# A decoder layer with seven-product matrix multiplication: sums of weights made ahead of time for one more pair of chunks

## The chip, the cores and the metric

The kernel runs on one core of one Trainium2 chip. The metric is the device time of one execution in microseconds (us), as the median of several runs; lower is better. A profile is one further execution, recorded instruction by instruction. The engines of the core are TensorE (PE: matmuls; PEld: its weight loads), VectorE (DVE), ScalarE (ACT), GpSimd (POOL) and SyncE (SP, which here only issues transfers).

## The reference

One layer over 256 tokens of width 2048, all in float32: a SwiGLU feed-forward (inner width 5632), a token mixer, a cross-attention, a second SwiGLU feed-forward, a final norm.

```python
def swiglu(h, w_gate, w_up, w_down):
    return (jax.nn.silu(h @ w_gate) * (h @ w_up)) @ w_down

...
x = x + 0.5 * swiglu(rms_norm(x, ffn1_norm[l]), ffn1_w_gate[l], ffn1_w_up[l], ffn1_w_down[l])
x = gated_parallel_mixer(x, ...)      # window attention || RWKV-7 time mixing
x = memory_cross_attention(x, ...)
x = x + 0.5 * swiglu(rms_norm(x, ffn2_norm[l]), ffn2_w_gate[l], ffn2_w_up[l], ffn2_w_down[l])
...
# in the time mixing:
kk = k * k_k
kk = kk / jnp.maximum(jnp.sqrt(jnp.sum(kk * kk, axis=-1, keepdims=True)), 1e-12)   # removal keys
```

## The kernel before

**Products of split numbers.** Every large product has float32 operands. Each operand is split into a high part, rounded to the fast matmul type (float32r), and a low part, what is left; a product is three matmuls: high x high, low x high, high x low (`times`, L417 to L419). For weights, ACT makes the high part (`hi`, L344) and VectorE the low part (`lo`, L345). TensorE holds 128 x 128 of the activations and streams 512 columns of weights.

**Items.** Weights come in items of `KU` = 2 chunks of 128 rows by 512 columns. `weight_plan` lists all of them in the order of use; `next_item` loads ahead (`load`, L336, on SP's queue), splits two items ahead (`divide`) and hands over the next. In the mixer a load is 512 KB, into one of four `raw` tiles; in the feed-forwards it is 1024 KB (`raw2`, also four).

**Seven products.** Gate and up of the same 512 columns, or two column blocks of down, are done together (`product_pair`). A pair of chunks, two column blocks and two token blocks make a 2 x 2 by 2 x 2 block product: eight products plainly, seven in the Strassen-Winograd way, with sums of activations (`combinations`) and sums of weights. `SEVEN = (0, 2, 4)` says that of the eight pairs of chunks of a gate-and-up block, the pairs 0, 2 and 4 are done with seven. For those, `divide` makes four differences on VectorE (L371 to L374) into two `raw` tiles, and splits them (`two_parts`, L352 on ACT, L353 on VectorE) into `thi`/`tlo`, of which there is one set for the first sum and one for the second. One row of the up weights is then not needed by itself.

The second feed-forward has one gate-and-up block done plainly (j = 0) and ten later ones done in pairs, in three groups of columns, each followed by its down products.

**The mixer** runs a fixed list of products (queries, keys, the small vectors, removal and attention gates, receptances and values, the late gates, then the projections), and between their matmuls the steps of background generators: `product` calls `bg.tick()` twice per item, and each tick lets the first generators of each group take one step to their next `yield`. `idle(n)` is n ticks of waiting. `removal_keys` sums squares over a head with a full-precision matmul by `bdones` (L1022), `substitute` solves small triangular systems step by step on VectorE, `pairs` is the chain of masked products (L1190 to L1306), `finish` makes the features `yr` that the product by `w_proj_rwkv` needs. Large mixer tiles come from one ring of 23, `t4`: a new tile waits until the tile that had its place is done with.

**Order.** Instructions of each engine run in the order in which they stand in the program. That order is fixed when the program is made, by a scheduler that follows the order above and moves an instruction ahead of another that it expects to wait. A transfer on SP's queue waits for its own semaphores, and everything behind it on that queue waits too.

Of the kernel before, what the change touches and what calls it, by code (L numbers as in the profile page):

```python
# [7 lines left out]
F32 = mybir.dt.float32  # L8
# [27 lines left out]


SEVEN, SEVEN_DOWN = (0, 2, 4), ((2, 4, 6), (2, 4))


# [40 lines left out]
def feed_forward_plan(wg, wu, wd, last):  # L81
    for j0, nj in GROUPS:
        for j in range(j0, j0 + nj):
            if j == 0:
                for w in (wg, wu):
                    yield w, 0, KD, 0, 512
            else:
                yield (wg, wu), 0, KD, (j * 512, j * 512), SEVEN
        yield (wd, wd), 4 * j0, 4 * nj, (0, 512), SEVEN_DOWN[nj < 4]
        if last and (j0, nj) == GROUPS[-1]:  # L90
            for n in (2, 3):
                yield wd, 4 * j0, 4 * nj, n * 512, 512
        else:
            yield (wd, wd), 4 * j0, 4 * nj, (1024, 1536), SEVEN_DOWN[1]
# [38 lines left out]
def decoder_layer(ctx: ExitStack, tc: tile.TileContext, a: dict, out: bass.AP):  # L133
# [15 lines left out]
    bg.group("norm", 1)  # L149
    bg.group("mem", 1)  # L150

    def f32(x):
# [34 lines left out]
    select(ident[:], ones[:], [[-1, P]], ALU.is_equal, 0.0, 0, 1)  # L187
    bdup = cpool.tile([P, 2, P], F32, name="bdup")[:, 0, :]
    center = cpool.tile([P, P], F32, name="center")

    def mixer_constants(sp):

        abias = sp.tile([P, 2, P], F32, name="abias")
        pool.memset(abias[:], 0.0)
        select(abias[:, 0, :], abias[:, 0, :], [[1, P]], ALU.is_gt, NEG, 0, -1)
        select(abias[:, 1, :], abias[:, 1, :], [[-1, P]], ALU.is_ge, NEG, 0, 1)

        ups = sp.tile([P, 2, P], F32, name="ups")[:, 0, :]
# [7 lines left out]
        select(mask_l[:], ups, [[-1, P]], ALU.is_gt, 0.0, 0, 1)  # L206
        bdones = sp.tile([P, P], F32, name="bdones")
# [3 lines left out]
        pool.memset(bdup, 0.0)  # L211
# [6 lines left out]
        keep = sp.tile([P, 2, P], F32, name="keep")  # L218
# [7 lines left out]
        return abias, mask3, mask_l, bdones, ones_r, keep  # L226

# [73 lines left out]

    plan, units, items, ends = [], [], [], []
    for entry in weight_plan(a):
        if entry is None:
            ends.append(len(units))
            continue
        plan.append(entry)
        w, k0, nk, c0, n = entry
        if not isinstance(w, tuple):
            for k in range(k0, k0 + nk, KU):  # L310
                items.append(((len(units),), False))
                units.append((w, k, c0, n))
            continue
        for k in range(k0, k0 + nk, 2 * KU):
            u = len(units)
            units += [(v, k + i, c, 512) for v, c in zip(w, c0) for i in (0, KU)]
            items += [((u + i, u + 2 + i), (k - k0) // KU + i in n) for i in range(2)]
    raws, parts = {}, {}
# [37 lines left out]
    def divide(i):  # L356
# [14 lines left out]
        dve.tensor_tensor(t[1][:, 0], ru[:, 0], rg[:, 0], ALU.subtract)  # L371
        dve.tensor_tensor(t[0][:, 0], ru[:, 1], ru[:, 0], ALU.subtract)
        dve.tensor_tensor(t[0][:, 1], ru[:, 1], t[1][:, 0], ALU.subtract)  # L373
        dve.tensor_tensor(t[1][:, 1], rg[:, 1], t[0][:, 1], ALU.subtract)  # L374
        a_ = two_parts(t[0], "a")
        parts[i] = split_unit(g), split_unit(u, slice(1, 2)), (a_, two_parts(t[1], "b"))

    def next_item():
# [7 lines left out]
        for j in range(i + 1, min(i + 1 + AHEAD, len(items))):  # L386
# [3 lines left out]
            for v in items[j][0]:  # L390
                load(v)
            divide(j)
        return parts[i]

# [33 lines left out]

    def combinations(sp, x: Act, seven, name, ready=lambda: True, early=True):

        pairs = [q for q in range(max(seven) + 1) if early or q in seven]
        n = 12 if not early else sum(4 if q in seven else 2 for q in pairs)
        parts = [sp.tile([P, n, P], F32R, tag=name + e, name=name + e) for e in ("hi", "lo")]
# [222 lines left out]
    def feed_forward(sp, x, norm: Norm, wg, wu, wd, done, begin_last=lambda: None, last=False):  # L658
        if last:
# [8 lines left out]
        c = combinations(  # L668
            sp, norm.x, SEVEN, "c", lambda: norm.r is not None and at["item"] > begun + 4
        )  # L670
        c["next"] = []
        for gi, (j0, nj) in enumerate(GROUPS):
# [3 lines left out]
            )  # L676
            ch = combinations(sp, h, SEVEN_DOWN[nj < 4], "d", early=False)

# [93 lines left out]
    with tc.tile_pool(name="mx", bufs=1, reuse_waits="tile") as sp:  # L772
        aligned(sp)
        abias, mask3, mask_l, bdones, (bdones_r, bdmean), keep = mixer_constants(sp)
# [233 lines left out]
        def removal_keys(h):  # L1008
# [8 lines left out]
            act.activation(sq[:], kk[:], AF.Square)  # L1017
            yield
            for i in (0, 2):
                b = tr()  # L1020
                sq2 = sq[:, i : i + 2, :].rearrange("p c t -> p (c t)")
                pe.matmul(b[:], bdones[:], sq2, start=True, stop=True)  # L1022
                act.activation(sq2, b[:], AF.Sqrt)
# [28 lines left out]
            for c in range(2):  # L1052
# [81 lines left out]
        def values(h):  # L1134
# [13 lines left out]
            for i in (0, 2):  # L1148
                b = head_sums(
                    bdones_r, [v[:, i : i + 2, :].rearrange("p c t -> p (c t)") for v in kp[h]]  # L1150
                )
# [51 lines left out]
        def pairs(h, q):  # L1203
# [11 lines left out]
            for c in range(2):  # L1215
                cs_ = slice(c * P, (c + 1) * P)
                if c == 0:
                    mk = masked(h, js, ((0, 0), (1, 0)))
                    yield
                    later = masked(h, js, ((2, 0), (2, 1)))  # L1220
                    yield
                vp = [vtok[h][:, c, j * P : (j + 1) * P] for j in js]
# [85 lines left out]
                if c == 0:  # L1308
                    s0 = small("s0", "s0", 2)
                    for k, j in enumerate(js):  # L1310
                        dve.scalar_tensor_tensor(
                            s0[:, k, :], b[:, (2 + k) * P : (3 + k) * P], dec[h][:, j : j + 1],
                            bdup, ALU.mult, ALU.mult,
                        )
# [100 lines left out]
        for n in range(4):  # L1415
# [4 lines left out]
            for t in range(2):  # L1420
                dve.tensor_tensor(s[:, t, :], po[t][:], s[:, t, :], ALU.add)
            bg.spawn("feat", n3.block(n, s))
            if n == 0:
# [156 lines left out]
```

## Time and profile before

| | us |
|---|---|
| median of 3 runs | 2251.75 |
| lowest and highest run | 2251.66, 2252.43 |
| the profiled execution | 2252.57 |
| its span, first to last instruction | 2250.8 |

The granted TensorE clock over the span is 0.999. By place in the span, the first feed-forward ends near 745 us, the mixer and the cross-attention near 1520, the second feed-forward with the final norm ends the span. The transfers move 432.49 MB at a mean of 192 GB/s.

In the page's and the views' lines, a row of instructions reads: engine, line of the kernel, operation, output tile `<-` input tiles, shapes, count; then busy time and mean of one. In an order by time, the row begins with its start and its duration in us, and brackets give the idle time of the engine before it and what ended it. Matmuls overlap in the pipe, so their durations are longer than the distance of their starts.

### The profile page before, as it was taken

How to read it: one execution, taken by the hardware profiler on the slowest of the kernel's cores; microseconds unless marked ns; L12 is line 12 of the kernel's file. 1: busy time of each engine (PE TensorE's matmuls, PEld its weight loads, DVE VectorE, ACT ScalarE, POOL GpSimd, SP SyncE). 2: the span in 40 equal slices, each digit the busy share in tenths (PEclk: the TensorE clock that was granted, in tenths of full speed). 3: DMA queues.
4: the chain of work that ended last, by engine and by line, in shares of the span. 5: the costliest groups of instructions: out<-in, count | busy, mean ns of one | idle time of the engine just before them, and what ended most of it. 6: DMA issues, size and time to landing. Idle time of an engine off the chain costs nothing.

```text
span 2250.8 us, 28046 instructions
## 1 busy us (share of the span) xinstructions
PE 2235.2 (99%) x10617; PEld 1840.3 (82%) x10617; DVE 1782.0 (79%) x2279; ACT 1226.5 (54%) x1601; POOL 132.6 (6%) x192
## 2 busy tenths in 40 slices
PE   9999999999999999999999999999999999999998
PEld 7888888888888877788888888888888888888886
DVE  7898988998989476887534566557998988998987
ACT  6555555555556467444444446556555555554554
POOL 1000000000001000301220040001000000000002
PEclk9999999999999999999999999999999999999999
DMA  7555555556556544676523476548565565555564
GB/s 263 187 201 201 197 203 202 193 190 216 192 188 205 163 142 150 201 223 212 166 77 109 163 261 227 186 159 284 185 213 187 195 210 194 190 209 200 189 207 147
DMA packets 219143, 432.49 MB, mean 192 GB/s; under 512 B 14107, under 2 KB 16384, under 8 KB 219008
## 3 DMA queue, kind: packets, MB, share of 16 engines
q1 hardware_dynamic: 210432, 404.78, 53.3%
q0 software_dynamic: 8112, 25.12, 3.5%
q8 instruction: 83, 1.36, 0.2%
q10 hardware_dynamic: 464, 0.79, 0.1%
q14 instruction: 52, 0.43, 0.1%
HBM read 417.56 MB, written 13.11 MB: 191 GB/s over the span
## 4 chain that ended last, share of the span: by engine, by line
PE 94%; DVE 3%; DMA 1%; issue 1%; POOL 1%; ACT 0%; SPq 0%; POOLq 0%; DVEq 0%; ACTq 0%
PE acc L417 19%; PE acc L418 19%; PE acc L419 19%; PE mm L419 8%; PE mm L418 8%; PE mm L417 8%; PE tr L605 2%; PE tr L418 2%; PE tr L419 2%; PE tr L417 2%; PE mm L1254 1%; DVE lo L345 1%; PE tr L1190 1%; DMA raw<-in_w_out_dram 0%; PE mm L844 0%
## 5 line engine op out<-in xcount | busy, mean ns | idle before, releaser
L345 DVE TENSOR_TENSOR lo<-raw,hi 128x1024 fp32r<-128x1024 f32 (+1 forms) x770 | 894.5, 1163 | 336.6 <-ACT hi L344 334.4
L344 ACT CAST hi<-raw 128x1024 fp32r<-128x1024 f32 (+1 forms) x770 | 759.3, 997 | 734.7 <-PE acc L419 519.6
L417 PE MATMUL acc<-hi,xhi 128*128 128x512 f32 (+1 forms) x1196 | 474.3, 397 | 2.4 <-ACT xhi L632 1.9
L418 PE MATMUL acc<-lo,xhi 128*128 128x512 f32 (+1 forms) x1196 | 464.8, 389 | 0.0
L419 PE MATMUL acc<-hi,xlo 128*128 128x512 f32 (+1 forms) x1196 | 464.1, 388 | 0.0
L417 PEld LDWEIGHTS acc<-hi,xhi 128*128 128x128 f32 x1196 | 225.0, 188 | 51.4 <-issue 4.0
L419 PEld LDWEIGHTS acc<-hi,xlo 128*128 128x128 f32 x1196 | 224.5, 188 | 46.9 <-DVE xlo L633 1.0
L418 PEld LDWEIGHTS acc<-lo,xhi 128*128 128x128 f32 x1196 | 224.9, 188 | 45.3 <-issue 1.7
L352 ACT CAST thi<-raw 128x1024 fp32r<-128x1024 f32 x172 | 178.9, 1050 | 60.4 <-DVE raw L373 46.5
L353 DVE TENSOR_TENSOR tlo<-raw,thi 128x1024 fp32r<-128x1024 f32 x172 | 208.3, 1220 | 0.7 <-ACT thi L352 0.4
L417 PE MATMUL mm<-hi,xhi 128*128 128x512 f32 x380 | 149.3, 393 | 0.0
L419 PE MATMUL mm<-hi,xlo 128*128 128x512 f32 x380 | 148.2, 390 | 0.0
L418 PE MATMUL mm<-lo,xhi 128*128 128x512 f32 x380 | 148.2, 390 | 0.0
L418 PE MATMUL acc<-lo,hhi 128*128 128x512 f32 x372 | 145.6, 391 | 0.8 <-DVE lo L345 0.8
L419 PE MATMUL acc<-hi,hlo 128*128 128x512 f32 x372 | 145.6, 391 | 0.0
L417 PE MATMUL acc<-hi,hhi 128*128 128x512 f32 x372 | 144.9, 390 | 0.0
L419 PEld LDWEIGHTS mm<-hi,xlo 128*128 128x128 f32 x380 | 71.3, 188 | 14.8
L418 PEld LDWEIGHTS mm<-lo,xhi 128*128 128x128 f32 x380 | 71.4, 188 | 14.5
L417 PEld LDWEIGHTS mm<-hi,xhi 128*128 128x128 f32 x380 | 71.4, 188 | 14.5
L418 PEld LDWEIGHTS acc<-lo,hhi 128*128 128x128 f32 x372 | 69.9, 188 | 15.5 <-DVE lo L345 1.2
L417 PEld LDWEIGHTS acc<-hi,hhi 128*128 128x128 f32 x372 | 69.9, 188 | 14.3
L419 PEld LDWEIGHTS acc<-hi,hlo 128*128 128x128 f32 x372 | 69.9, 188 | 14.0
(392 smaller groups left out, 3511.9 us busy)
## 6 DMA issues: line engine op xcount, KB each, us to landing
raw<-in_ffn_w_up_dram SPq DMA_DIRECT2D x88, 1024.0 KB, 5.4
raw<-in_ffn_w_down_dram SPq DMA_DIRECT2D x88, 1024.0 KB, 5.1
raw<-in_ffn_w_gate_dram SPq DMA_DIRECT2D x84, 1024.0 KB, 5.1
raw<-in_w_in_dram SPq DMA_DIRECT2D x136, 512.0 KB, 3.5
raw<-in_w_out_dram SPq DMA_DIRECT2D x32, 512.0 KB, 4.5
raw<-in_w_proj_attn_dram SPq DMA_DIRECT2D x16, 512.0 KB, 3.9
raw<-in_w_proj_rwkv_dram SPq DMA_DIRECT2D x16, 512.0 KB, 5.7
raw<-in_w_cross_kv_dram SPq DMA_DIRECT2D x16, 512.0 KB, 3.6
```

Of the source, the lines that this page charges most:

```text
L344: at["hi"] = act.copy(hi[:, s], raw[:, s])
L345: at["lo"] = dve.tensor_tensor(lo[:, s], raw[:, s], f32(hi[:, s]), ALU.subtract)
L352: act.copy(hi[:], v[:])
L353: dve.tensor_tensor(lo[:], v[:], f32(hi[:]), ALU.subtract)
L417: pe.matmul(o, xh, hi, start=first, stop=False, **how)
L418: pe.matmul(o, xh, lo, start=False, stop=False, **how)
L419: pe.matmul(o, xl, hi, start=False, stop=last, **how)
L605: pe.transpose(b[:, o : o + P], tok[:, t, col : col + P], ident[:])
L1190: pe.matmul(b[e][:, o : o + P], x1[r, j, cs_], x2[r, j, cs_], start=True, stop=True)
L1254: pe.matmul(vb[:, (o + k) * P : (o + k + 1) * P][:, r], lhs(k, e), rhs[:, k, r], start=first and k + e == 0, stop=True, **ek,)
```

## The change

Four things are changed.

- In the second feed-forward, the ten later gate-and-up blocks use seven products in the pairs 0, 2, 3 and 4 (`SEVEN_2`) instead of 0, 2 and 4. The sums of activations (`combinations`) grow by two blocks.
- For pair 3 the sums of weights are not made there. Ten generators (`stage`, a background group of its own, up to four at a time), which start during the receptance, value and late gate products at the items in `STAGE_AT`, load the pair's gate and up weights into two `t4` tiles, make the four differences on VectorE, and store the sums to device memory, all transfers on SP's queue. In the second feed-forward `load_sums` brings them back into two `raw` tiles, two items ahead. The row of the up weights that is not used is not loaded.
- `removal_keys` splits the squares (`halves_of`, new tiles `sh` and `sl`) and sums them with the two matmuls of `head_sums` by the float32r `bdones`.
- Steps of the mixer are delayed by ticks (`idle`, `later_by`): the small vectors' shifts, the removal keys, `substitute`, the masks of `pairs`, the norm after `w_out`; the last attention projection does its last items one token block after the other (`skew`); some constants move between pools.

```diff
+SEVEN_2, STAGED = (0, 2, 3, 4), (3,)
+STAGE_AT = [257, 261, 265] + [268 + 2 * n for n in range(7)]
...
-                yield (wg, wu), 0, KD, (j * 512, j * 512), SEVEN
+                yield (wg, wu), 0, KD, (j * 512, j * 512), SEVEN_2 if last else SEVEN
...
+    bg.group("stage", 4)
...
+    def later_by(n, steps):
+        yield from idle(n)
+        yield from steps
...
+            for i in range(2):
+                q = (k - k0) // KU + i
+                if n == SEVEN_2 and q in STAGED:
+                    staged[len(items)] = len(staged)
+                items.append(((u + i, u + 2 + i), q in n))
+    first_unused = {items[i][0][1] for i in staged}
+    sums_d = dram.tile([len(staged), P, 4, 512], F32, name="sums")
...
+        if u in first_unused:
+            second = u + 1 in first_unused
+            pieces = [(slice(1, 2), nc.sync)] + [(slice(2 + second, 4), nc.sync)]
+            if not second:
+                pieces = ((slice(1, 4), nc.sync),)
+        elif u + 1 in first_unused and wide:
+            pieces = ((slice(0, 2), nc.sync), (slice(3, 4), nc.sync))
...
+    def load_sums(i):
+        if i not in staged or i in summed:
+            return
+        summed[i] = [
+            wp.tile([P, KU, 512], F32, tag="raw", name="raw", bufs=4) for _ in range(2)
+        ]
+        for e, t in enumerate(summed[i]):
+            nc.sync.dma_start(t[:], sums_d[staged[i], :, KU * e : KU * e + KU, :])
+
+    def stage(t4, i, n):
+        while at["item"] < STAGE_AT[n]:
+            yield
+        t = t4("su", (P, KU, 512)), t4("sg", (P, KU, 512))
+        for e, v in zip(t, items[i][0][::-1]):
+            w, k, c0, _ = units[v]
+            rows = slice(k * P, (k + KU) * P)
+            nc.sync.dma_start(e[:], w[rows, c0 : c0 + 512].rearrange("(a p) n -> p a n", p=P))
+        yield from idle(4)
+        u0, u1, g0, g1 = (e[:, c] for e in t for c in range(KU))
+        with tc.issue_after(at["lo"].ins):
+            dve.tensor_tensor(g0, u0, g0, ALU.subtract)
+            dve.tensor_tensor(u0, u1, u0, ALU.subtract)
+        yield
+        with tc.issue_after(at["lo"].ins):
+            dve.tensor_tensor(u1, u1, g0, ALU.subtract)
+            dve.tensor_tensor(g1, g1, u1, ALU.subtract)
+        yield from idle(6)
+        for c, e in enumerate(t):
+            nc.sync.dma_start(sums_d[n, :, KU * c : KU * c + KU, :], e[:])
...
-        rg, ru = raws[g], raws[u]
-        t = [wp.tile([P, KU, 512], F32, tag="raw", name="raw", bufs=4) for _ in range(2)]
+        t = summed.get(i)
+        if t is None:
+            rg, ru = raws[g], raws[u]
+            t = [wp.tile([P, KU, 512], F32, tag="raw", name="raw", bufs=4) for _ in range(2)]
...
             for v in items[j][0]:
                 load(v)
+            load_sums(j)
             divide(j)
+        load_sums(i + 2)
...
+        for i, n in staged.items():
+            bg.spawn("stage", stage(t4, i, n))
...
+            if name == "small":
+                yield from idle(2)
...
-            yield
+            sp_ = halves_of(sq[:], t4("sh", dt=F32R)[:], t4("sl", dt=F32R)[:])
+            yield from idle(2)
             for i in (0, 2):
-                b = tr()
                 sq2 = sq[:, i : i + 2, :].rearrange("p c t -> p (c t)")
-                pe.matmul(b[:], bdones[:], sq2, start=True, stop=True)
+                b = head_sums(
+                    bdones, [v[:, i : i + 2, :].rearrange("p c t -> p (c t)") for v in sp_]
+                )
...
                 pool.dma_start(ld[:, o : o + 8, :], lt[:])
-                yield
+                yield from idle(2)
...
         def substitute():
-            yield from idle(4)
+            yield from idle(10)
...
-            pa = product(ya, W["w_proj_attn"])
+            pa = product(ya, W["w_proj_attn"], skew=n == 3)
...
                     later = masked(h, js, ((2, 0), (2, 1)))
-                    yield
+                    yield from idle(2)
...
                     mk_next = masked(h, js, ((0, 1), (1, 1)))
-                    yield
+                    yield from idle(2)
...
-            bg.spawn("feat", n3.block(n, s))
+            bg.spawn("feat", later_by(2, n3.block(n, s)))
```

More of the change, by code (lines that the diff above doesn't have):

```diff
@@ L187, in decoder_layer @@
     select(ident[:], ones[:], [[-1, P]], ALU.is_equal, 0.0, 0, 1)
-    bdup = cpool.tile([P, 2, P], F32, name="bdup")[:, 0, :]
-    center = cpool.tile([P, P], F32, name="center")
+    cpool.tile([P, P], F32, name="shift")
     def mixer_constants(sp):
@@ L196, in mixer_constants @@
         select(abias[:, 1, :], abias[:, 1, :], [[-1, P]], ALU.is_ge, NEG, 0, 1)
-        ups = sp.tile([P, 2, P], F32, name="ups")[:, 0, :]
+        keep = sp.tile([P, 2, P], F32, name="keep")
+        ups = keep[:, 0, :]
         pool.memset(ups, UP)
@@ L206, in mixer_constants @@
         select(mask_l[:], ups, [[-1, P]], ALU.is_gt, 0.0, 0, 1)
+        bdup = sp.tile([P, P], F32, name="bdup")
+        center = sp.tile([P, P], F32, name="center")
         bdones = sp.tile([P, P], F32, name="bdones")
@@ L210, in mixer_constants @@
         pool.memset(bdmean[:], 0.0)
-        pool.memset(bdup, 0.0)
+        pool.memset(bdup[:], 0.0)
         for e in range(2):
@@ L217, in mixer_constants @@
         pool.tensor_tensor(center[:], ident[:], bdmean[:], ALU.subtract)
-        keep = sp.tile([P, 2, P], F32, name="keep")
         pool.memset(keep[:], 1.0)
@@ L225, in mixer_constants @@
             ones_r.append(r)
-        return abias, mask3, mask_l, bdones, ones_r, keep
+        return abias, mask3, mask_l, bdup, center, ones_r, keep
     sinks = cpool.tile([P, 16], F32, name="sinks")
@@ L297, in decoder_layer @@
     junk_t = cpool.tile([P, 512], mybir.dt.bfloat16, name="junk")
-    plan, units, items, ends = [], [], [], []
+    plan, units, items, ends, staged = [], [], [], [], {}
     for entry in weight_plan(a):
@@ L316, in decoder_layer @@
             units += [(v, k + i, c, 512) for v, c in zip(w, c0) for i in (0, KU)]
-            items += [((u + i, u + 2 + i), (k - k0) // KU + i in n) for i in range(2)]
-    raws, parts = {}, {}
+            for i in range(2):
[3 more added lines that the diff above has]
+                items.append(((u + i, u + 2 + i), q in n))
+    raws, parts, summed = {}, {}, {}
+    first_unused = {items[i][0][1] for i in staged}
+    sums_d = dram.tile([len(staged), P, 4, 512], F32, name="sums")
     at = {"item": 0, "product": 0, "pool": None}
@@ L427, in multiply, with combinations @@
             )
-    def combinations(sp, x: Act, seven, name, ready=lambda: True, early=True):
+    def combinations(sp, x: Act, seven, name, ready=lambda: True, early=True, n=0):
         pairs = [q for q in range(max(seven) + 1) if early or q in seven]
-        n = 12 if not early else sum(4 if q in seven else 2 for q in pairs)
+        n = n or sum(4 if q in seven else 2 for q in pairs)
         parts = [sp.tile([P, n, P], F32R, tag=name + e, name=name + e) for e in ("hi", "lo")]
@@ L668, in feed_forward @@
         c = combinations(
-            sp, norm.x, SEVEN, "c", lambda: norm.r is not None and at["item"] > begun + 4
+            sp, norm.x, SEVEN_2 if last else SEVEN, "c", lambda: norm.r is not None and at["item"] > begun + 4
         )
@@ L676, in feed_forward @@
             )
-            ch = combinations(sp, h, SEVEN_DOWN[nj < 4], "d", early=False)
+            ch = combinations(sp, h, SEVEN_DOWN[nj < 4], "d", early=False, n=12)
             def transposed(hb, c):
@@ L773, in decoder_layer @@
         aligned(sp)
-        abias, mask3, mask_l, bdones, (bdones_r, bdmean), keep = mixer_constants(sp)
+        abias, mask3, mask_l, bdup, center, (bdones, bdmean), keep = mixer_constants(sp)
         def t4(name, shape=(P, 4, T), dt=F32):
             return sp.tile(list(shape), dt, tag="t4", name=name, bufs=N4)
+        for i, n in staged.items():
+            bg.spawn("stage", stage(t4, i, n))
         def act_tiles(name, n):
@@ L1149, in values @@
                 b = head_sums(
-                    bdones_r, [v[:, i : i + 2, :].rearrange("p c t -> p (c t)") for v in kp[h]]
+                    bdones, [v[:, i : i + 2, :].rearrange("p c t -> p (c t)") for v in kp[h]]
                 )
@@ L1312, in pairs @@
                             s0[:, k, :], b[:, (2 + k) * P : (3 + k) * P], dec[h][:, j : j + 1],
[L1313 removed]
+                            bdup[:], ALU.mult, ALU.mult,
                         )
```

8 lines of the change are left out of this document (4 added, 4 removed).

## The prediction

> **What bounds the kernel now.** I read the page first, then the busy time by stretches, then single instructions.
>
> ```profile
> span 2250.8 us, 28046 instructions
> PE 2235.2 (99%) x10617; PEld 1840.3 (82%) x10617; DVE 1782.0 (79%) x2279; ACT 1226.5 (54%) x1601; POOL 132.6 (6%) x192
> PE 94%; DVE 3%; DMA 1%; issue 1%; POOL 1%; ACT 0%; SPq 0%; POOLq 0%; DVEq 0%; ACTq 0%
> ```
>
> TensorE is busy for 99% of the span and carries 94% of the chain that ended last. So a matmul removed anywhere is time removed, and any new wait of TensorE is time added. Where the other engines have room is seen by stretch (us; then busy us and instructions of PE, PEld, DVE, ACT, POOL; granted clock, DMA share, GB/s):
>
> ```profile
> 850.00:1000.00 150.00, 149.70 (x705) 118.96 (x705) 117.47 (x159) 83.12 (x106) 23.37 (x21) 1.00 0.62 195
> 1069.00:1124.00 55.00, 54.69 (x303) 45.84 (x302) 32.15 (x37) 26.07 (x32) 16.40 (x25) 1.00 0.55 166
> 1124.00:1165.00 41.00, 41.00 (x325) 37.11 (x325) 13.52 (x21) 14.15 (x27) 14.08 (x22) 1.00 0.28 85
> 1700.00:1900.00 200.00, 200.00 (x890) 165.10 (x889) 182.70 (x222) 109.60 (x121) 0.00 (x0) 1.00 0.58 200
> ```
>
> In the second feed-forward (1700 to 1900) VectorE is at 182.7 of 200 us: little room. From 1069 to 1165, the receptance, value and gate products, it has 45.7 of 96, and the DMA engines are half idle. The granted clock is 1.00 throughout, so it enters no term.
>
> **The main term: 30 matmuls.** A pair of chunks costs eight products of three matmuls plainly and seven with sums; ten blocks turn their fourth pair, so 10 x 3 = 30 matmuls of 128x512 go. The pace, not the listed 0.39 us, is the price, as matmuls overlap:
>
> ```profile
> 1810.04 0.39 PE L417 MATMUL acc<-hi,xhi 128*128 128x512 f32 x1
> ...
> 1822.73 0.39 PE L419 MATMUL acc<-hi,xlo 128*128 128x512 f32 x1
> ```
>
> There are 56 steps between these rows: 12.69 / 56 = 0.2266 us. **30 x 0.2266 = 6.80 us gained.**
>
> **Removal keys.** Four full-precision matmuls become eight of the split kind:
>
> ```profile
> 887.68 1.02 PE L1022 MATMUL tr<-sq,bdones 128*128 128x512 f32 x2
> 888.14 0.80 PE L417 MATMUL acc<-hi,xhi 128*128 128x512 f32 x1
> 888.78 0.40 PE L418 MATMUL acc<-lo,xhi 128*128 128x512 f32 x1
> ```
>
> From the start of the first row to the third 1.10 us pass, of which an ordinary matmul takes 0.2266: 0.87 each. 4 x 0.87 - 8 x 0.2266 = **1.67 us gained**. The two new casts and two new low parts (two of 1.05 on ACT, two of 1.13 on VectorE, a table load of 1.28) lie in 850 to 1000, where ACT has 67 of 150 us free and VectorE 33, behind the plain weight products; uncovered they would cost some 6 us, but the key steps now idle two ticks for them.
>
> **Delays of background steps.** They aim at the few waits TensorE has (idle time and releaser in brackets):
>
> ```profile
> 816.16 0.33 PE L605 MATMUL tr<-ident,tok 128*128 128x128 f32 x1 [0.75 <-ACT tok L788]
> 1018.68 0.39 PE L419 MATMUL acc<-hi,xlo 128*128 128x512 f32 x1
> 1019.49 0.50 PE L417 MATMUL acc<-hi,xhi 128*128 128x512 f32 x1 [0.43 <-DVE ga L1112]
> 1111.39 1.08 PE L1190 MATMUL tr<-rt,kk 64*128 64x128 f32 x8 [0.31 <-DVE mk L1196]
> 1364.70 0.33 PE L605 MATMUL tr<-ident,x 128*128 128x128 f32 x1 [0.71 <-DVE x L1421]
> 1365.30 0.55 PE L605 MATMUL tr<-ident,x 128*128 128x128 f32 x3 [0.27 <-DVE x L1421]
> ```
>
> The idle times add to 2.47 us. From start to start the second wait cost 0.81 - 0.23 = 0.58, 0.15 more than its idle time; five times that gives 3.2. Bounds 0 (each wait returns a step later) and 3.2; I take **2.8 gained**, nearer to the rows, as each delay passes at least six matmuls (1.36 us), more than any of these waits.
>
> **Staging: VectorE and queues.** Each of ten stages adds two loads of 512 KB, four differences and two stores. A difference costs its pace:
>
> ```profile
> 1809.09 0.69 DVE L374 TENSOR_TENSOR raw<-raw,raw 128x512 f32<-128x512 f32 x1
> 1809.70 1.22 DVE L345 TENSOR_TENSOR lo<-raw,hi 128x1024 fp32r<-128x1024 f32 x1
> 1810.83 1.22 DVE L353 TENSOR_TENSOR tlo<-raw,thi 128x1024 fp32r<-128x1024 f32 x1
> ```
>
> 0.61 for 512 columns, 1.13 for 1024. 40 x 0.61 = 24 us, into a stretch where VectorE has 50 free; nothing by itself. The forty DMAs are the risk, because SP is one queue and the weights stand behind them. In the changed program's order, from the second staged pair to a weight load of the second late gate block, for which TensorE waits at once, 36 DMAs follow each other: 12 staged loads, 10 stores, 14 weight loads. Between the same points TensorE has 210 weight matmuls (47.6 us) and 36 small ones; from 1124 to 1165, where small ones prevail, 325 records take 41 us, 0.126 each, and many are two records, so these are some 5.5: 53 us. What a full queue delivers:
>
> ```profile
> 5.00:25.00 20.00, 18.07 (x87) 13.67 (x86) 12.78 (x20) 15.09 (x31) 0.00 (x0) 1.00 1.04 387
> 1290.00:1340.00 50.00, 50.00 (x234) 41.40 (x233) 30.59 (x31) 22.39 (x26) 15.17 (x14) 1.00 0.79 268
> raw<-in_w_in_dram SPq DMA_DIRECT2D x136, 512.0 KB, 3.5
> 1815.26 0.39 PE L419 MATMUL mm<-hi,xlo 128*128 128x512 f32 x1
> 1815.68 1.05 ACT L344 CAST hi<-raw 128x1024 fp32r<-128x1024 f32 x1 [2.05 <-PE mm L419]
> ```
>
> At 387 GB/s a DMA of 524288 bytes takes 1.355 us; scaled from 0.79 to a full share the second row gives 268 / 0.79 = 339 GB/s, 1.55 us. With 3.5 - 1.36 = 2.1 us from last byte to landing and 1.05 for the cast, the weights are ready after 36 x 1.355 + 3.2 = 52.0 us: one us early. But the tiles of the stores are reused: ACT's copy of a gate sum (L1382's tile) waits for the 41st DMA, 41 x 1.355 + 2.1 = 57.7, and ends at 58.4, where TensorE asks 56.5 (53 + 6 matmuls + 8 small ones + 0.5 for the masks): 1.9 late, and weight casts queue behind it on ACT. At 1.55 the same point is at 66.4: 10 late. Bounds 0 and 10; **2.4 lost**, near the first row, which is the same queue with the same 2 KB rows, a little more because 10 of the 36 are stores, which no saturated row shows.
>
> The Trainium skill, page "DMA: Bandwidth & Descriptors", section "Where 436 GB/s comes from", has it that the HBM side, about 358 GB/s, binds such transfers. The row of 5 to 25 us shows 387, so here the measurement decides; by 358 (1.46 us) the 41st DMA would land 4.3 us later and the sum, as an estimate, would end near 2250.
>
> **The mixer's chain.** Delays put its first masked products 120 TensorE instructions later: ten weight items, 10 x 12 x 0.2266 = 27 us. It had this room:
>
> ```profile
> 1262.59 0.62 PE L802 MATMUL tr<-sp,ones_r 128*128 128x512 f32 x2
> 1272.36 0.61 ACT L610 CAST yrhi<-yq 128x512 fp32r<-128x512 f32 x1
> 1273.00 0.69 DVE L611 TENSOR_TENSOR yrlo<-yq,yrhi 128x512 fp32r<-128x512 f32 x1 [1.18 <-ACT yrhi L610]
> L417 PE MATMUL acc<-hi,yrhi x64: 387/389/482, 1293.4 to 1339.1; 128*128 128x512 f32 x64
> ```
>
> The last yrhi is used three items (8.2 us) after 1293.4, so 1301.6 - 1273.7 = 28 us were spare, and 1 is left. From the sums (L802) to yrhi 10.4 us pass; the changed order holds 39 matmuls and four of L1349 (0.41 each) there, 10.5 us, but two weights' low parts (1.13 each) stand among the VectorE steps. Bounds 0 and 1.5; **0.7 lost**. Where loads are late, the order puts chain steps with 3 instead of 6 matmuls between them (0.68 us against some 0.42 + 0.37 + 0.1 for a step through ACT), about ten times: bounds 0 and 4, **1.5 lost**.
>
> **Second feed-forward.** Pairs 2, 3 and 4 now stand back to back, with one set of tiles for the sums' parts. Per block VectorE gains 3 x 1.13 + 0.61 - 2 x 1.13 = 1.7 us and TensorE sheds 0.68. A block is 183 matmuls and eight transposes, 42.2 us; at 182.7 / 200 VectorE has 38.6 of it, then 40.3 of 41.5: 97%. I lay the changed order along the block, time zero at its first product, an ACT cast starting 0.42 after the matmul that it waits for (rows of 1815). Pair 2 ends at 14.95, so the second staged sum is cast from 15.14 to 16.19; its low part holds VectorE to 17.7, three differences and a half low part to 20.1, a gate's low part to 21.2, the low part of pair 4's first sum to 22.46. It is first used by matmul 99, at 22.43; the other's at 23.59 for matmul 104, at 23.57. Late by under 0.1: **0.6 lost in ten blocks**, bounds 0 and 15 (below). The loaded sums (two of 512 KB) are issued some 8 us ahead of a 3.5 us landing.
>
> **Sum.** -6.80 - 1.67 - 2.8 + 2.4 + 1.5 + 0.7 + 0.6 = -6.1 us. Against the profiled execution's 2252.57 that is 2246.5; it stands 0.8 above the median of the runs, 2251.75, so **2245.7**. Constants moved between pools, and gates' skewed order beyond the 0.43 above, cost nothing.
>
> **Rivals.**
> *The gain arrives whole.* Loads and stores overlap and the late copies find their landing done: -6.80 - 1.67 - 2.8 = -11.3, **2240.5**. For it: 387 GB/s at 1.04 share. Against: ACT's new waits on stores.
> *The queue is full.* At 339 GB/s TensorE waits 10 instead of 2.4: **2253.3**, no change. For it: the mixed stretch at 0.79. Against: it was not full.
> *Slower: VectorE becomes the bound of the ten blocks.* Place: the low parts of pair 4's sums. Price: each us by which they are late is paid ten times, for 97% leaves 1.2 us a block to catch up. From 1.1 us late a block it is slower than before; at 1.5 it is 2245.7 - 0.6 + 15 = **2260**. For it: the margin of zero above. Against: casts that wait for TensorE stand before low parts now too (1815.68), and from 1700 to 1900 TensorE waits for none.
> That the ten pairs don't shrink is excluded: the program holds 30 weight matmuls fewer.
>
> **How the numbers follow.** Forecast (2242 to 2249.5) 0.50; whole gain 0.13; full queue (2249.5 to 2254.5) 0.23; VectorE 0.14. Range 2239.8 to 2254.5: the first three. 0.2% is 4.5 us, what a measurement of this kernel can tell from no change: faster below 2247.2, slower above 2256.3. Faster 0.13 + 0.46 + 0.02 = 0.61; same 0.04 + 0.21 = 0.25; slower 0.14.
>
> **What would show it.** PE busy some 8 us less; in each of the ten blocks about 41.5 instead of 42.2 us from block to block with no wait of L418 on tlo above 0.2; in the mixer waits of TensorE on ACT behind stores of sums, 2 to 3 us in all, and DMA near 350 GB/s there; the waits on tok, ga, mk and x gone. Wrong it is if TensorE waits over 6 us in the staging stretch or over 0.5 us in each block, or if the waits that the delays aim at come back elsewhere.

## The result, and where the time went

The changed kernel takes 2265.17 us (median of 4 runs, 2263.23 to 2266.93) against 2251.7 for the kernel before on the same chip: ratio 1.0059, 95% interval 1.0046 to 1.0071. It is 13.5 us slower where 6 us faster was forecast, and 10.7 above the end of the stated range (2254.5).

The page after, three lines that answer to those of before:

```profile
span 2261.5 us, 28255 instructions
PE 2234.5 (99%) x10587; PEld 1833.5 (81%) x10587; DVE 1829.0 (81%) x2344; ACT 1248.0 (55%) x1624; POOL 131.0 (6%) x192
PE 93%; DMA 2%; DVE 2%; issue 1%; ACT 1%; SPq 0%; POOLq 0%; POOL 0%; ACTq 0%; DVEq 0%
```

The 30 matmuls are gone (10617 to 10587), yet PE is busy 0.7 us less, not 8, and the span is 10.7 us longer. So matmuls became slower somewhere, and TensorE waits elsewhere. The waits of TensorE by line, the longest of them last in each row:

```profile
PE acc L477 <- ACT hi L400: 6.0, 3, 3.1
PE acc L478 <- DVE lo L401: 4.5, 5, 2.1
PE acc L477 <- ACT xhi L692: 2.3, 2, 1.5
PE mm L1126 <- DVE lt L1132: 1.4, 1, 1.4
PE acc L477 <- ACT gr L1449: 0.5, 1, 0.5
```

The first row did not exist before: weights' high parts are late, and the second was 0.8. The place is seen by stretches (columns as in the prediction: us; busy us and instructions of PE, PEld, DVE, ACT, POOL; granted clock, DMA share, GB/s):

```profile
850.00:1000.00 150.00, 145.18 (x688) 116.16 (x687) 116.53 (x146) 85.36 (x108) 20.76 (x21) 1.00 0.62 190
940.00:960.00 20.00, 17.80 (x94) 13.88 (x93) 20.00 (x22) 6.79 (x7) 6.16 (x4) 1.00 0.53 159
1095.00:1160.00 65.00, 58.05 (x268) 45.97 (x268) 45.63 (x57) 23.93 (x28) 18.71 (x26) 0.92 1.01 355
1143.00:1154.00 11.00, 7.40 (x19) 4.55 (x21) 7.64 (x9) 2.19 (x3) 0.00 (x0) 0.55 1.04 342
1700.00:1900.00 200.00, 200.00 (x892) 164.30 (x891) 185.90 (x230) 113.83 (x126) 0.00 (x0) 1.00 0.60 205
```

TensorE idles in two places: 850 to 1000 (145.2 busy, 149.7 before), with VectorE full from 940 to 960, and 1095 to 1160, where the DMA engines stand at 1.01 for 65 us. Inside the second the granted clock falls to 0.55. From 1700 to 1900, in the second feed-forward, TensorE has no idle time. The matmuls around the lowest clock, in order of time:

```profile
1139.72 0.40 PE L479 MATMUL acc<-hi,xlo 128*128 128x512 f32 x1
1143.25 0.51 PE L477 MATMUL acc<-hi,xhi 128*128 128x512 f32 x1 [3.13 <-ACT hi L400]
1144.51 0.80 PE L478 MATMUL acc<-lo,xhi 128*128 128x512 f32 x1 [0.75 <-DVE lo L401]
1145.11 0.63 PE L479 MATMUL acc<-hi,xlo 128*128 128x512 f32 x1
1145.53 0.63 PE L477 MATMUL acc<-hi,xhi 128*128 128x512 f32 x1
1145.96 0.63 PE L478 MATMUL acc<-lo,xhi 128*128 128x512 f32 x1
1146.39 0.63 PE L479 MATMUL acc<-hi,xlo 128*128 128x512 f32 x1
1149.08 0.80 PE L477 MATMUL acc<-hi,xhi 128*128 128x512 f32 x1 [2.06 <-ACT hi L400]
```

After a wait of 3.13 us the matmuls step by 0.43 us instead of 0.227: this wait is paid again by slow matmuls behind it. What ScalarE waited for between 1095 and 1300, and the transfers between 1095 and 1160 (size, median us from issue to landing):

```profile
ACT hi L400 <- DMA raw<-in_w_in_dram: 27.4, 7, 6.0
ACT gr L1449 <- DMA sums<-sg: 4.8, 1, 4.8
```

```profile
DMA packets 10478, 23.11 MB, mean 355 GB/s; under 512 B 915, under 2 KB 947, under 8 KB 10475
raw<-in_w_in_dram SPq DMA_DIRECT2D x17, 512.0 KB, 11.0
sums<-su SPq DMA_DIRECT2D x6, 512.0 KB, 11.0
```

A weight load lands 11.0 us after its issue (3.5 in the whole span before): weights queue behind staged loads and stores. The account is best read from the starts of the same products in both kernels. The products that the table below uses, in the changed kernel (shortest, median, longest ns; first to last start):

```profile
L477 PE MATMUL acc<-hi,yahi x64: 388/389/398, 898.8 to 1020.8; 128*128 128x512 f32 x64
L477 PE MATMUL acc<-hi,yrhi x64: 387/389/582, 1306.4 to 1355.7; 128*128 128x512 f32 x64
L477 PE MATMUL acc<-hi,ochi x32: 387/389/578, 1529.0 to 1553.2; 128*128 128x512 f32 x32
```

How much later each such start is than in the kernel before (us, profiled executions; a is the first and b the last product by `ya`, c the first masked product `tr<-at,aa` of the chain, d the last product by `yr`, e the last cross-attention product by `oc`, f the last transposes of `hb`). The time is the median of the runs, the ratio that to the kernel before on the same chip, with its 95% interval. The profiled execution of the changed kernel took 2263.2, 2 us under its median, that of e2 2260.1, 3 above:

| kernel | a | b | c | d | e | f | time | ratio |
|---|---|---|---|---|---|---|---|---|
| changed | -1.6 | 4.0 | 29.0 | 16.6 | 15.6 | 10.3 | 2265.2 | 1.0059 (1.0046 to 1.0071) |
| e1_no_staging | -1.4 | 5.7 | 30.6 | 5.6 | 5.1 | 1.0 | 2253.5 | 1.0008 (0.9998 to 1.0017) |
| e2_mixer_only | -1.3 | 8.8 | 33.7 | 8.7 | 8.1 | 7.5 | 2257.0 | 1.0027 (1.0017 to 1.0037) |
| e3_spread | -1.2 | 6.0 | 30.8 | 9.4 | 9.5 | 4.6 | 2257.3 | 1.0028 (1.0016 to 1.0039) |
| e4_staging_only | 0.2 | 0.2 | 0.2 | 5.0 | 4.8 | 0.1 | 2252.6 | 1.0004 (0.9995 to 1.0014) |
| e5_keys_only | -0.8 | 3.7 | 6.2 | 4.2 | 3.9 | 3.4 | 2255.8 | 1.0017 (1.0007 to 1.0027) |
| e6_delays_only | -0.4 | -0.2 | 21.8 | 0.0 | -0.4 | -1.0 | 2252.3 | 1.0002 (0.9993 to 1.0011) |
| e7_staged_in_chain | -1.4 | 5.7 | 30.6 | 10.7 | 9.6 | 5.0 | 2258.6 | 1.0031 (1.0019 to 1.0043) |
| e8_best | -0.4 | -0.4 | -0.4 | -0.4 | -0.9 | -6.1 | 2246.6 | 0.9977 (0.9967 to 0.9986) |
| e10_keys_full | -0.1 | -0.8 | 21.7 | 18.4 | 18.1 | 13.0 | 2266.6 | 1.0065 (1.0050 to 1.0080) |
| e11_solve_early | -1.2 | 1.4 | 20.7 | 13.0 | 13.1 | 8.7 | 2261.3 | 1.0041 (1.0026 to 1.0055) |
| e12_keys_no_ticks | -0.8 | -1.0 | -1.0 | -1.0 | -1.1 | -1.6 | 2251.6 | 0.9999 (0.9990 to 1.0009) |
| e13_best_keys | -1.1 | -1.3 | -1.3 | -1.2 | -1.4 | -6.7 | 2246.1 | 0.9972 (0.9961 to 0.9983) |
| e14_staged_later | -1.4 | 7.3 | 32.2 | 7.2 | 7.2 | 2.5 | 2255.0 | 1.0012 (1.0003 to 1.0022) |
| e15_later_no_ticks | -1.1 | -1.8 | 20.2 | 0.9 | 0.7 | -4.2 | 2248.2 | 0.9983 (0.9973 to 0.9992) |
| e16_no_ticks | -1.3 | -2.1 | 20.5 | 16.7 | 16.3 | 12.0 | 2265.8 | 1.0060 (1.0045 to 1.0075) |

The changed kernel gains 1.6 up to a, loses 5.5 from a to b, 12.7 from b to d, and gains 1.0 from d to e and 5.2 from e to f.

Of the 5.2, 0.5 to 0.7 are not the change's. e2, e5, e6 and e12, whose second feed-forward is that of before, gain as much from e to f: the profiled execution of the kernel before lost it there. From 1965.7 to 2117.4 it takes 151.7 us where its other column group and those of e2 take 151.1, and TensorE steps late at 2095 and at 2101, there by 0.24 (kernel before):

```profile
2100.73 0.39 PE L417 MATMUL tr<-thi,chi 128*128 128x512 f32 x1
2101.20 0.50 PE L418 MATMUL tr<-tlo,chi 128*128 128x512 f32 x1
```

So the turned pairs gain some 4.6.

### The profile page after: what moved, and what is told of

The parts are those of the page before. It is cut to its first block, busy times and chain, and to the rows that moved or that the text cites. A ratio compares the mean times of both kernels' runs of the same rounds, so it can differ in the third digit from the quotient of the medians.

```text
span 2261.5 us, 28255 instructions
## 1 busy us (share of the span) xinstructions
PE 2234.5 (99%) x10587; PEld 1833.5 (81%) x10587; DVE 1829.0 (81%) x2344; ACT 1248.0 (55%) x1624; POOL 131.0 (6%) x192
## 4 chain that ended last, share of the span: by engine, by line
PE 93%; DMA 2%; DVE 2%; issue 1%; ACT 1%; SPq 0%; POOLq 0%; POOL 0%; ACTq 0%; DVEq 0%
PE acc L477 18%; PE acc L478 18%; PE acc L479 18%; PE mm L478 8%; PE mm L479 8%; PE mm L477 8%; PE tr L665 2%; PE tr L478 2%; PE tr L477 2%; PE tr L479 2%; PE mm L1321 1%; DMA raw<-in_w_in_dram 1%; DVE lo L401 1%; PE tr L1257 1%; ACT hi L400 0%
## 5 line engine op out<-in xcount | busy, mean ns | idle before, releaser
L477 PE MATMUL acc<-hi,xhi 128*128 128x512 f32 (+1 forms) x1166 | 461.8, 397 | 9.3 <-ACT hi L400 6.0
L478 PE MATMUL acc<-lo,xhi 128*128 128x512 f32 (+1 forms) x1166 | 454.2, 390 | 3.4 <-DVE lo L401 3.4
L479 PE MATMUL acc<-hi,xlo 128*128 128x512 f32 (+1 forms) x1166 | 453.8, 390 | 0.0
L477 PEld LDWEIGHTS acc<-hi,xhi 128*128 128x128 f32 x1166 | 219.7, 188 | 58.0 <-ACT hi L400 7.6
L478 PEld LDWEIGHTS acc<-lo,xhi 128*128 128x128 f32 x1166 | 219.8, 188 | 47.4 <-DVE lo L401 5.7
L479 PEld LDWEIGHTS acc<-hi,xlo 128*128 128x128 f32 x1166 | 219.4, 188 | 46.0 <-DVE xlo L693 1.0
L408 ACT CAST thi<-raw 128x1024 fp32r<-128x1024 f32 x192 | 199.7, 1051 | 61.8 <-DVE raw L431 41.3
L409 DVE TENSOR_TENSOR tlo<-raw,thi 128x1024 fp32r<-128x1024 f32 x192 | 232.0, 1218 | 1.2 <-ACT thi L408 0.4
```

Source lines behind the costliest of these rows:

```text
L408: act.copy(hi[:], v[:])
L409: dve.tensor_tensor(lo[:], v[:], f32(hi[:]), ALU.subtract)
L477: pe.matmul(o, xh, hi, start=first, stop=False, **how)
L478: pe.matmul(o, xh, lo, start=False, stop=False, **how)
L479: pe.matmul(o, xl, hi, start=False, stop=last, **how)
```

## Experiments: which part costs what

**One part away, or one part alone.** The first four take staging out (the second feed-forward then reads plain weights in place of the sums, so e1 does not compute the layer), leave only the mixer's edits, move staging far back, and add staging without the mixer's edits.

```diff
 # e1: the changed kernel
-            bg.spawn("stage", stage(t4, i, n))
...
-            nc.sync.dma_start(t[:], sums_d[staged[i], :, KU * e : KU * e + KU, :])
+            nc.sync.dma_start(t[:], w[rows, c0 : c0 + 512].rearrange("(a p) n -> p a n", p=P))
 # e2: the changed kernel
-SEVEN_2, STAGED = (0, 2, 3, 4), (3,)
+SEVEN_2, STAGED = (0, 2, 4), ()
 # e3: the changed kernel
-STAGE_AT = [257, 261, 265] + [268 + 2 * n for n in range(7)]
+STAGE_AT = [300 + 8 * n for n in range(10)]
 # e4: the changed kernel, removal_keys and every idle, later_by and skew as before
-                    bdones, [v[:, i : i + 2, :].rearrange("p c t -> p (c t)") for v in sp_]
+                pe.matmul(b[:], bd32, sq2, start=True, stop=True)
```

> The changed kernel without the ten staged sums in the mixer: the second feed-forward loads plain weights of the same bytes in their place, so those sums are left out of the result; all else is as changed. Theory A (queue): the 12.6 us that the changed kernel loses between the end of the ga products and the end of the yr products (+4.0 us late at 1021, +16.6 at 1356) are the staged transfers filling the SP queue; without them 2265.2 - 12.6 = 2252.6, with no TensorE wait over 1 us between 1100 and 1200. Theory B (delays): they are the chain's delays, which put its steps behind too few matmuls; staging gives 3 us at most, so 2262, and the chain's stretch stays as long. Both: from 740 to 1021 it stays some 4.6 us longer than before, and the second feed-forward 5.3 us shorter.

> Only the mixer's edits (removal keys' sums in split form, delays, constants); the second feed-forward turns three pairs as before, nothing is staged. Theory A (queue): +4.6 up to 1021, -1.0 from the delay ahead of the cross-attention's norm, nothing else: 2251.7 + 3.6 = 2255.3. Theory B (delays): the loss of the chain's stretch stays but for 3 us: 2265.2 + 5.3 - 3 = 2267.5. The prediction's own terms for these edits (-1.67 - 2.8 and 2.2 lost in the chain) would give 2249.4.

> The changed kernel with its ten staged sums started at weight items 300, 308, ... 372 instead of 257 to 280: the receptance gates' products, the output products and the cross-attention's, where the DMA engines are at some 0.65. Theory A (queue): each sum's four transfers (2 MB, 5.4 us at 387 GB/s) now have eight items, 22 us; the 12.6 us are saved but for 1 to 2: 2253 to 2255. Theory B (delays): 2262 or more.

> The kernel before with the ten staged sums and four turned pairs alone: removal keys' sums in full precision and every delay as before. Theory A (queue): 2251.7 + 12.6 - 5.3 = 2259.0, with the waits for staged transfers between 1100 and 1200. Theory B (delays): 2251.7 + 3 - 5.3 = 2249.4. Both: up to 1021 as before, with no VectorE at 10 of 10 us between 940 and 960.

e1: 2253.5, theory A. From b to d it is as long as the kernel before (5.6 - 5.7 = -0.1), the changed kernel 12.7 longer: staging costs 12.8 us there. One row of the stretches of e1 shows the difference; the changed kernel's row for the same 100 us stands under it:

```profile
1100.00:1200.00 100.00, 99.69 (x656) 85.84 (x654) 44.71 (x52) 43.53 (x64) 19.64 (x27) 1.00 0.45 136
```

```profile
1100.00:1200.00 100.00, 92.68 (x565) 77.24 (x563) 63.27 (x82) 36.34 (x52) 17.00 (x24) 0.95 0.87 300
```

e2 (2257.0, near A's 2255.3) has the whole loss from a to b, 10.1 there, without any staging. e3 (2257.3) moves staging away from 1140 and loses 3.6 more than e1 between b and d, most of it in one wait of 3.0 on `yrhi`, so its 300 to 372 is no free place either. e4 is theory A's miss: 2252.6 instead of 2259. Staging at the same items costs 4.8 when the mixer's order is that of before, and 12.8 when the changed mixer's order is there. The two parts are worse together than the sum of both (+0.7 and +5.2 apart, +13.5 together), so a third theory was needed: the items in `STAGE_AT` count weights, not time. The mixer's edits put the chain's small products 29 us later (column c; 21.8 by the delays alone, e6), and the weight items 256 to 276 then follow each other in 60 us (e3, counted by the weights' products) instead of 102 in the kernel before.

**Keys and delays apart; staging put among the chain's products.**

```diff
 # e5: the kernel before with the removal keys' edit alone; e6: with the delays alone
 # e7: the changed kernel; e8: e4 and two of the delays (small vectors, norm after w_out)
-STAGE_AT = [257, 261, 265] + [268 + 2 * n for n in range(7)]
+STAGE_AT = [272 + 2 * n for n in range(10)]    # e7
+STAGE_AT = [268 + 2 * n for n in range(10)]    # e8
```

> The kernel before with the removal keys' sums in split form alone (two casts, two low parts, eight matmuls, two idle ticks in each half's steps), no delays, nothing staged. Theory K (keys): the later key steps bunch VectorE's work, it stands at 10 of 10 us around 940 to 960, and weights' low parts come late: from 898 to 1021 the stretch grows by some 3 us and the time is 2251.8 - 1.7 + 3 = 2253. Theory D (delays): the growth of 5.5 to 10 us there is the substitution's, whose loads and VectorE steps start six ticks later; then 2251.8 - 1.7 = 2250.1 here.

> The kernel before with all delays alone: removal keys in full precision, nothing staged. Theory K (keys): 2251.8 - 0.6 (tok) - 0.9 (x) + 2.5 (the wait near 990 behind the substitution's loads) = 2252.8. Theory D (delays): 898 to 1021 grows by 5.5 or more: 2256 or more.

> The changed kernel with its ten staged sums started at weight items 272, 274, ... 290, which is where the delayed chain now runs: items 272 to 292 take 134 us, items 257 to 278 took 58. Theory C (collision): the staged transfers cost 12.8 us because the delays took the chain's small products out of the stretch into which they were put; set back among them they cost 3 at most: 2265.2 - 10 = 2255. Theory V (volume): the queue is full wherever they stand in the mixer: 2262 or more.

> Four turned pairs with ten staged sums started at items 268, 270, ... 286, among the chain's products as they stand in the kernel before, with two delays (the small features', the cross norm's) and none of the rest: removal keys in full precision. By theory C: 2251.8 - 5.2 (second feed-forward) - 0.6 - 0.9 + 1 = 2246. By theory V: 2251.8 - 6.7 + 5 = 2250 or more.

e5 (2255.8) loses 4.5 from a to b, e6 (2252.3) 0.2: theory K, with more than its 3 us. e8 is 5.2 us faster than the kernel before (2246.6, theory C's 2246): staging costs nothing from b to d. Its transfers from 1110 to 1290 move at 230 GB/s and weights land in 3.8 us:

```profile
1110.00:1290.00 180.00, 179.69 (x1216) 155.76 (x1216) 111.49 (x142) 79.85 (x125) 22.93 (x37) 1.00 0.68 230
```

```profile
raw<-in_w_in_dram SPq DMA_DIRECT2D x27, 512.0 KB, 3.8
```

e7 was to come to 2255 and took 2258.6: from b to d staging still costs 5.2 against e1. What VectorE waits for there is not weights, but tiles of the ring `t4` whose last user is a store that has not landed:

```profile
DVE mk L1263 <- DMA sums<-sg: 4.5, 2, 3.1
DVE mk L1263 <- DMA sums<-su: 4.1, 1, 4.1
```

Its first two stages stand ahead of the delayed chain, and the chain's masks take their tiles.

**The two ticks, and the order of loss.**

```diff
 # e10: the changed kernel, removal keys in full precision and without their ticks
 # e11: the changed kernel
-            yield from idle(10)     # substitute
+            yield from idle(4)
 # e12: e5;  e13: e8 with the removal keys' edit;  e16: the changed kernel
             sp_ = halves_of(sq[:], t4("sh", dt=F32R)[:], t4("sl", dt=F32R)[:])
-            yield from idle(2)
+            yield
```

> The changed kernel with the removal keys' sums back in full precision and without their two extra ticks; staging and delays as changed. Theory C (collision): up to 1021 it is no longer than before (-5 against the changed kernel); the other delays alone put the chain 22 us later instead of 29, so the staged transfers still meet plain weights and cost 8 to 12: 2257 to 2260. Theory K (keys): the keys are behind all of it; then 2251.8 - 0.4 - 5.3 + 4.8 (staging among the chain's products) = 2251.

> The changed kernel with one delay undone: the triangular solve starts four ticks after the removal keys instead of ten. Theory C (collision): the chain then starts some 7 to 9 us later than before instead of 29, the staged transfers run among its products and cost 5 instead of 12.8, and the solve's loads stand where they did, so the wait of 2.3 near 990 goes too: 2255 to 2257. If the staged transfers cost the same wherever the chain is: 2262 or more.

> The kernel before with the removal keys' sums in split form, without the two extra ticks in each half: the low parts stand one tick ahead of their sums. Theory T (ticks): the two ticks, not the low parts, put the key steps and with them the solve's loads later on the SP queue, where weights stand behind them; without them the four matmuls' gain arrives: 2251.8 - 1.7 = 2250.1, and no wait over 1 us near 973. Theory L (low parts): the two casts and two low parts are what VectorE and ScalarE have no room for: 2253 or more.

> The version with the staged sums started at items 268, 270, ... 286 and two delays (2246.6), with the removal keys' sums in split form and no extra ticks. Theory T: 2246.6 - 1.7 = 2244.9. Theory L: 2248 or more.

> The changed kernel without the removal keys' two extra ticks alone, staging where it was. Theory T (ticks): up to 1021 it is 5 us earlier than the changed kernel, the staged transfers still meet plain weights: 2265.2 - 5 = 2260. If the ticks are not the cause beside the delays: 2263 or more.

e12 settles the keys: the same split sums without the ticks lose nothing from a to b (-0.2, e5 4.5), theory T in the trace; the runs (2251.6) can't tell its 1.6 from no change. Where the ticks hurt in e5 is SP's queue. The transfers of e5 (with ticks), then of e12:

```profile
937.52 19.86 SPq L359 DMA_DIRECT2D raw<-in_w_in_dram  x7
963.80 2.35 SPq L1143 DMA_DIRECT2D dl<-ld  x4
966.25 2.44 SPq L359 DMA_DIRECT2D raw<-in_w_proj_attn_dram  x4
```

```profile
938.34 16.62 SPq L359 DMA_DIRECT2D raw<-in_w_in_dram  x6
959.35 3.73 SPq L1143 DMA_DIRECT2D dl<-ld  x4
963.17 0.51 SPq L359 DMA_DIRECT2D raw<-in_w_in_dram  x1
963.78 6.70 SPq L359 DMA_DIRECT2D raw<-in_w_proj_attn_dram  x4
```

The solve's loads (`dl`) wait at the head of the queue for the stores of `ld`; the ticks make these later, so in e5 the weights behind are issued 2.5 us later (966.25 instead of 963.78) and TensorE waits 1.7 us for them; behind that wait matmuls step by 0.43 us again (granted clock 0.83 from 970 to 980). The changed kernel has the same ticks and another place of loss, as `substitute` is delayed there too. Its transfers:

```profile
961.90 7.89 SPq L359 DMA_DIRECT2D raw<-in_w_proj_attn_dram  x4
971.99 0.37 SPq L359 DMA_DIRECT2D raw<-in_w_in_dram  x1
972.57 5.78 SPq L1147 DMA_DIRECT2D dl<-ld  x4
```

The solve's loads come after these weights and hold none of them up. VectorE is full instead (20.00 of 20 from 940 to 960, 17.99 in e16), and `lt` and weights' low parts come late: TensorE waits 2.5 us for low parts, 1.4 for `lt`, 0.8 for high parts and 0.5 for `ga` between 898 and 1025, in e16 0.2 in all.

e10, e11 and e16 missed upwards: 2266.6, 2261.3 and 2265.8 where 2257 to 2260, 2255 to 2257 and 2260 were expected. e16 is 6.0 earlier than the changed kernel at b and level with it at d. Undoing one delay (e11) left the chain 20.7 late, not 8, so the other delays move it as well, and 11.6 are lost from b to d. With the chain 20 to 22 late the store of a staged sum holds a tile that ScalarE's copy of `vtok` needs. TensorE in e16, then what ScalarE waited for:

```profile
1145.64 0.39 PE L479 MATMUL acc<-hi,xlo 128*128 128x512 f32 x1
1155.29 1.97 PE L1294 MATMUL tr<-vtok,mk 128*128 128x64 f32 x8 [9.26 <-ACT vtok L1213]
```

```profile
ACT vtok L1213 <- DMA sums<-su: 12.7, 1, 12.7
```

So what is won ahead of the full queue is lost in it, by another wait.

**Place and ticks together.**

```diff
 # e14: the changed kernel; e15: the same without the two ticks
-STAGE_AT = [257, 261, 265] + [268 + 2 * n for n in range(7)]
+STAGE_AT = [278 + 2 * n for n in range(10)]    # e14
+STAGE_AT = [276 + 2 * n for n in range(10)]    # e15
```

> The changed kernel with its ten staged sums started at weight items 278, 280, ... 296, all behind the first of the delayed chain's products (item 276), with a stage in every second item. Theory P (place): staging hidden as in the version with 268 to 286 among the early chain; what is left is as without staging: 2252 to 2254, and no wait of VectorE, ScalarE or TensorE on a stored sum. Theory O (something else of the delayed order): 4 or more lost between 1021 and 1356 against the version without staging: 2257 or more.

> The changed kernel without the removal keys' two extra ticks and with its staged sums started at items 276, 278, ... 294. If place and ticks are the two losses: 2251.8 - 1.7 - 0.6 - 0.9 - 5.3 = 2243.3 at best; the solve's delay may keep its wait near 990, 2.5: 2246. If the delays lose something of their own: 2250 or more.

e14: from b to d -0.1, as without staging, and no computing engine waits there for a stored sum: so place decides, and the volume, ten times 2 MB, is hidden where the chain's products stand around it. Its 2255.0, between the two theories' times, is the loss from a to b, 8.7. e15 is faster than the kernel before (2248.2), by 4 of the 8.5 us of its best case; from b to d it loses 2.7. The delays alone do not lose that (e6, 0.2), nor do the delays with staging behind the chain (e14, -0.1); what does was not found. e13, without those delays, has the lowest time: 2246.1, 0.9972 of before, not told apart from e8.

## Why the prediction was wrong

*30 matmuls, 6.80, less 0.6 for low parts just in time.* Right in mechanism, 1.6 too much: from e to f the changed kernel gains 5.2, as e8 and e13 do, and 4.6 without the 0.6 that the kernel before lost there in its profile. From the first transposes of one block to those of the next it takes 42.0 to 42.1 us, 42.4 to 42.5 before, where 41.5 and 42.2 were worked out. No single wait on `tlo` is over 0.2, but there are more of them than the 0.6 allowed for. Weight loads wait for `tlo` in 13 places of the second feed-forward (two in e2), and there products start 0.3 us and more apart instead of 0.227:

```profile
1663.51 0.39 PE L477 MATMUL acc<-thi,xhi 128*128 128x512 f32 x1
1663.80 0.19 PEld L478 LDWEIGHTS acc<-tlo,xhi 128*128 128x128 f32 x1 [0.33 <-DVE tlo L409]
1663.81 0.50 PE L478 MATMUL acc<-tlo,xhi 128*128 128x512 f32 x1
```

Over the products with the sums' parts such steps add 1.8 us to those of e2, which is most of the 2.2 between 6.80 and 4.6. The rival that VectorE becomes the bound of the ten blocks (2260) is refuted: with 185.9 of 200 us busy it still kept up but for these steps.

*Removal keys, 1.67, and the sentence "the key steps now idle two ticks for them".* This step failed. The sums themselves gained 1.1 (e12 at d, -1.0, with 0.1 at the start). The ticks, named as the cover of the new casts, were the cost: at b the changed kernel is 6.0 later than e16. The prediction followed the casts and low parts, found room for them, and did not follow what the later steps hold up: in e5 the weights on SP's queue, in the changed kernel the low parts on VectorE. The loss does not add to the next one: e16, without the ticks, takes 2265.8, no less than the changed kernel.

*Delays, 2.8.* Measured 0.5 for `tok` and 0.4 for `x` (e6), none for the others, and 0.4 is lost again from a to d: 0.5 in all at e (-0.4, with 0.1 at the start). Their price was outside that list: the chain 21.8 us later.

*Staging, 2.4 with bounds 0 and 10.* This step failed by most: 12.8. The prediction had the queue, the 36 transfers in 53 us and both rates, and chose 387 GB/s from a row of 20 us with loads alone; over 65 us with stores among them the queue gave 355 at a share of 1.01. The 36 transfers in 53 us ask for 356, so nothing was spare. It had the weights ready 1 us early and one copy of ScalarE late; at 355 its own sum has them 3.4 us late (36 x 1.477 + 3.2 - 53, an estimate), and weights are what ScalarE waited for, 27.4 us in all against 4.8 for a store. By the Trainium skill, page "DMA: Bandwidth & Descriptors", section "Where 436 GB/s comes from", the HBM side binds at some 358 GB/s; the prediction set that aside for 387, and these 65 us agree with the page. That the HBM side is what binds them, no run here shows. The bound of 10 was passed by a term that the prediction left out ("it enters no term"), the granted clock. From 1100 to 1200 TensorE idles 7.0 us more than in e1, which is inside the bounds; its clock of 0.95 over these 100 us (0.55 from 1143 to 1154) makes up to 5 of the other 5.8 (an estimate).

*The mixer's chain, 1.5 and 0.7.* Nothing was lost there without staging (e1, b to d, -0.1).

*The rival "the queue is full", 2253.3,* named the mechanism. Put the measured sizes into its sum: queue 12.8 instead of 10, ticks 6.0, keys 0.6 short, delays 2.3 short, blocks 1.6 short, chain 2.2 saved: 2253.3 + 2.8 + 6.0 + 0.6 + 2.3 + 1.6 - 2.2 = 2264.4, 0.8 under the median. These sizes are read one after the other in the changed kernel; they are not what leaving one part out would save, as e16 shows. Of the 6.0 of the ticks, 5.0 are the waits on VectorE and ScalarE named above; the rest, and the 2.7 of e15, stay open.

## What to carry to other kernels

Background work tied to a count of items moves in time when another edit changes what stands between the items: price two such edits together, by bytes per microsecond in the stretch where they will run. A tick of delay is not free cover: follow what the delayed step stores, who loads it, what stands behind that load on its queue, and what its later work crowds on its engine. Transfers can be hidden behind small products (from 1124 to 1165 the kernel before has its DMA engines at 0.28) and lie open among plain weight products, which alone keep them at some 0.6 (850 to 1000).

## What had not been expected of the hardware

Short waits of TensorE can be paid twice, and not in every execution. The same wait, on `lt` before 957 (1.4 us), in two kernels that are alike up to there, left the clock at full in the changed kernel's profile and not in e2's:

```profile
955.00:965.00 10.00, 8.61 (x42) 6.88 (x41) 8.09 (x8) 2.92 (x3) 5.60 (x7) 1.00 0.81 255
```

```profile
955.00:965.00 10.00, 8.62 (x27) 6.74 (x27) 7.20 (x7) 1.25 (x2) 5.85 (x7) 0.66 0.77 252
```

In e2 and e14 some fifteen weight matmuls stepped by 0.43 us behind waits of 1.4 and 2.1 us, 3.0 us in all, which is most of why e2 is 4.8 later at b than the changed kernel. The runs of e1, e2 and e14 scatter over 4 to 6 us, while those of e8 and e13, with no wait over 0.8 in the mixer, scatter over some 2. The clock granted over a whole run goes with it: the changed kernel's four runs took 2263.2 and 2263.6 at 0.997, 2266.8 and 2266.9 at 0.996 and 0.995. No single wait under 1.1 us was followed by half-rate matmuls in these profiles. The Trainium skill, page "TensorE: Matmul & The Clock Gate", section "What's actually happening", ties the slow clock to an idle window of about 3.4 us that runs freely; that it differs from one execution to the next agrees with these traces, the length does not: 1.4 us was enough.
